# A two-layer block on one core: modulation parts ahead of the projection's first half, and two more dense steps ahead of each query chunk

## The chip, the cores and the metric

The kernel runs on one core of a Trainium2 chip. The metric is the time of one execution on the device, in microseconds. A core has TensorE (PE in the views), VectorE (DVE), ScalarE (ACT), GpSimd (POOL) and SyncE (SP), each with its own list of instructions; they wait for one another by semaphores. SP, POOL and ACT issue DMAs.

## The reference

Two transformer layers on 256 latent tokens with 256 context tokens beside them, 1024 wide, all in float32:

```python
for l in range(2):
    mx, mc = (silu(c) @ w_ada[l] + b_ada[l]), (silu(c_ctx) @ w_ada[l] + b_ada[l])   # 6 parts of 1024 each
    hx = rmsnorm(x, g0) * (1 + mx[1]) + mx[0]                                        # hc: the same with mc
    yx, yc = even_mixer(hx, hc) if l == 0 else odd_mixer(hx, hc)                     # attention, projections
    x = x + mx[2] * yx                                                               # layer 0: xc too
    h = rmsnorm(x, g1) * (1 + mx[4]) + mx[3]
    x = x + mx[5] * moe(h)                                                           # 16 experts, top 2
return rmsnorm(x, final_g)
```

Layer 0's mixer is a windowed attention (A) and a neighbourhood attention with a bias table (B), joined and multiplied by an output matrix. Layer 1's is an attention with normed and rotated queries and keys (C) and a long convolution, joined in the same way. The 6 modulation parts of a layer come from a 1024 x 6144 matrix, so they are mostly weight traffic.

## The kernel before

Each engine runs its instructions in the order in which the program writes them; nothing reorders them. The program is written as generators that are woven together: `weave(side, dense, r)` goes through an attention (`side`, two pauses per unit of 128 queries and two heads) and after each pause advances the dense work by r steps on average; `tick()` then moves on the delayed small work (`later`, and `turn_due`, which transposes a finished modulation part five ticks after its bias was added).

Weights come through `Stream W`: a list `specs` of 1 MB tiles in the order of their use, loaded by SP into a ring of 7; SP issues the next load when an older tile is used up. `order` of the list and order of the steps must agree.

The dense work beside the attentions is of three kinds. A modulation part (`g_ada`) has 4 tiles and 4 steps of 16 small matmuls; then VectorE adds the bias (`ab`, loaded by GpSimd, three buffers), GpSimd writes the row to DRAM (`mrow`) and TensorE transposes it (`adat`). An output projection (`g_out`, `op`) takes two tiles per half of its depth, 8 steps of 12 matmuls for four row tiles and two halves; each weight is split by ScalarE (high part) and VectorE (low part) and used in three products. Two weights of 512 columns fill one `pair` buffer; `Splits` keeps two ahead. The third kind are the narrow projections of layer 1's input (`qc` for the queries, `uh` for the convolution), 12 matmuls a step.

An attention unit goes: scores (`sB`, `sC`; for B also the bias table `E`), maxima and negation on VectorE (`mx`, `ng`), exponentials on ScalarE, then the scaling on VectorE, then the transposes (`tp`) of the unit before, copied out by ScalarE and VectorE (`pt`), and after the last unit of a chunk the sums (`oB`, `oC`).

In layer 0, `order_b` lists six modulation parts, (0,2), (0,4), (0,3), (0,5), (1,1), (1,0), as `ada_row(0)` to `ada_row(5)`. `fill` is the dense work beside attention B; `first` and `second` are the two halves of the projection; `ahead_first` and `ahead_out` only issue splits. After the attention follow the rest of the transposes, the shared rows of the router (`shw`), the second half of the projection, and the first expert stage (`moe`), which streams its weights.

In layer 1 each of four chunks of attention C calls `queries(c0)` first, which advances the dense work until that chunk's queries are stacked (`stackC`). Chunks 0 and 1 share one stack, and so do 2 and 3. Dense work there is: the query columns, a modulation part, the convolution's columns, `ada_row(2)`, the convolution's second half, the projection's first half, `ada_row(3)`.

Of the kernel before, what the change touches and what calls it, by code (L numbers as in the profile page):

```python
# [249 lines left out]
def tile_hybrid_flow(ctx, tc, xin, rows, adab, w_ada, w_in_e, w_out_e, sinkb, rpb, w_in_o, w_out_o, hyw,  # L250
# [50 lines left out]
    def xrow(i):  # L301

        return xt[i // 2][:, i % 2]
# [38 lines left out]
    def wtiles(ap, n, c, moe=0, kind="w"):  # L342

        return [wtile(ap, n, c, j, moe, kind) for j in range(ap.shape[1])]

    def ada_specs(l, parts, halves=(0, 1)):
        return sum([wtiles(w_ada[l], 512, 2 * q + h, kind="a") for q in parts for h in halves], [])
# [10 lines left out]
    def moe_specs(l):  # L358
        r = []
        for e in range(NE + 1):  # L360
            if e < NE:
                r += [sorted_tile(w, l, e, DE, j) for j in range(2) for w in (moe_wg, moe_wu)]
            if e:
                r += [sorted_tile(moe_wd, l, e - 1, D, j) for j in range(2)]
        return r
# [4 lines left out]
    wo = [[wtiles(w, 512, h) for h in range(2)] for w in (w_out_e, w_out_o)]  # L370
    wo = [[t[h][j] for j in range(2) for h in range(2)] for t in wo]
    specs = ada_specs(0, (1, 0), (0,)) + ada_specs(0, (1, 0), (1,))
# [1 line left out]
    specs += ada_specs(0, (2,))  # L374
    specs += ada_specs(0, (4,))
    specs += ada_specs(0, (3,))
    specs += wo[0][0:2]
    specs += ada_specs(0, (5,))
    specs += ada_specs(1, (1,))
    specs += ada_specs(1, (0,))  # L380
    specs += wo[0][2:4]
    specs += moe_specs(0)
    until_moe0 = len(specs)
    specs += cols(w_in_o, range(3)) + ada_specs(1, (2,), (0,)) + cols(w_in_o, (3,)) + ada_specs(1, (2,), (1,))
# [24 lines left out]
    def turn_due(at_once=False):  # L409

        for d in due:
            d[0] -= 1
        while due and (due[0][0] <= 0 or at_once):
            _, l, part, half, dst = due.pop(0)
            to, at = COLS[part]
            pt = tpt(f"adat{l}_{part}_{half}")
            T.transpose(pt[:, 0], dst, ident)
            V.tensor_copy(to[l][:, :, at, half * 4 : half * 4 + 4], pt[:, 0].rearrange("p (j v) -> p v j", v=32)[:, 0:2, :])
# [24 lines left out]
    def g_ada_row(order, n, pool, held):  # L443

        l, part, vs = order[n]
        for m in (n, n + 1):
            if m < len(order) and m not in held:
                if m > n:
                    turn_due(True)
                held[m] = ada_bias(*order[m][0:2], pool)  # L450
        yield from g_ada(l, part, pool, vs, bias=held.pop(n))
# [3 lines left out]
    def tick():  # L455

        for g in later[:2]:
            if next(g, later) is later:
                later.remove(g)
        turn_due()  # L460
# [9 lines left out]
    def weave(side, dense, r, whole=True):  # L470

        due = 0.0
        dense = iter(dense)
        for _ in side:
            due += r
            while due >= 1.0:
                due -= 1.0
                next(dense, None)
                tick()
        if whole:  # L480
            run(dense)

    def bcast(l, part, pool, vs, eng=G):
        t = pool.tile([P, len(vs), D], F32, name=f"bc{l}_{part}", tag=f"bc{part}")
        for a, v in enumerate(vs):
            eng.dma_start(t[:, a], mrow[l, part, v].partition_broadcast(P))
        return t
# [73 lines left out]
    class Splits:  # L561
# [25 lines left out]
        def next(self):  # L587
            self.fill()
            return self.queue.pop(0)
# [213 lines left out]
    def g_out(l, oh, ol, gate, tiles, ws, k0, lead=2):  # L803

        sp = ws if isinstance(ws, Splits) else Splits(ws, 512, lead, pool_lo=False)
        for half in range(2):
            hs = slice(half * 512, half * 512 + 512)
            grp = []
            for n, (i, ix, ig) in enumerate(tiles):
                ps = acc(f"op{l}_{half}_{k0}_{i}")  # L810
                tk = slice(i * P, i * P + P)
                for k in range(4):
                    if n == 0:
                        grp += sp.next()
                    _, hi, lo = grp[k]
                    mm3(ps, oh[k0 + k][:, tk], ol[k0 + k][:, tk], hi, lo, k == 0, k == 3)
                yield
                V.tensor_mul(ps, ps, gate(ig, half))
                V.tensor_add(xrow(ix)[:, hs], xrow(ix)[:, hs], ps)
# [798 lines left out]
    with tc.tile_pool(name="l0n", bufs=1, reuse_waits="tile") as pa:  # L1618
# [30 lines left out]
        fill = lambda n=1: [next(filters, None) for _ in range(n)]  # L1649
# [40 lines left out]
    with tc.tile_pool(name="l0q", bufs=1, reuse_waits="tile") as pq:  # L1690
# [48 lines left out]
        dense = []  # L1739
# [4 lines left out]
        dense = chain(*dense)  # L1744
# [31 lines left out]
        def chunk_b(c):  # L1776
            oh[4 + c], ol[4 + c] = htiles(pb, f"o{c}", 1, 512, f"oh{c}_") + htiles(pb, f"p{c}", 1, 512, f"ol{c}_")

            def bias(h, qt, ps):
                m0_ = 2 - 2 * (qt - 2)  # L1780
                T.matmul(ps[:, 256:512], ident, tabs[c][:, 7 * h + m0_ : 7 * h + m0_ + 4].rearrange("p m k -> p (m k)"), start=False, stop=True)

            return dict(nm=f"B{c}", q=qs[4 + c], k=ks[c], v=lambda kc, h: vB[:, kc, 128 * c + 64 * h : 128 * c + 64 * h + 64],
                        oh=oh[4 + c], ol=ol[4 + c], bias=bias, sink=None, qtiles=(0, 1, 2, 3), prep=lambda: bias_tab(c))
# [4 lines left out]
        def ada_row(n):  # L1789
            return g_ada_row(order_b, n, pe, held)  # L1790

        def reload():
            for i in range(4):
                SY.dma_start(xrow(i), xv[:, i])
            yield
# [8 lines left out]
        def ahead_first():  # L1804
            first.fill()
            yield

        def first_out():
            yield from g_out(0, oh, ol, gate0, [(i, i, i // 2) for i in range(4)], first, 0)
# [3 lines left out]
        def ahead_out():  # L1813
            second.fill()
            yield

        def gate_rows():
            gate[0] = bcast(0, 2, pb, (0, 1))
            yield

        fill = chain(ada_row(0), gate_rows(), ada_row(1), reload(), ada_row(2), ahead_first(), first_out(), ada_row(3), ada_row(4), ada_row(5), ahead_out())
        weave(g_attend(pq, [chunk_b(c) for c in range(4)]), fill, 1.26)
        turn_due(True)
    oactx.__exit__(None, None, None)
# [76 lines left out]
    with tc.tile_pool(name="l1n", bufs=1, side="right", reuse_waits="tile") as pa:  # L1901
# [27 lines left out]
        dense = chain(*[g_fm(sp, hh, hl, 256, ev_u(2 * j), f"u{j}") for j in range(4)])  # L1929
# [132 lines left out]
    def queries(c0):  # L2062

        while c0 not in stacked:
            next(dense)
            tick()

    order_c = [(1, part, (1,)) for part in (2, 4, 3, 5)]
    held = {}
# [7 lines left out]
    def fm(evac, c0, j, nm):  # L2077
        return g_fm(sp, hh, hl, 256, evac(c0 + 2 * j), f"{nm}{j}")
# [35 lines left out]
    dense = chain(g_kv(sp, hh, hl, ev_k, vt1, scr, "kvc"), fm(ev_q, 0, 0, "qc"), ada_row(1), fm(ev_q, 0, 1, "qc"), second_half())  # L2114
# [89 lines left out]
```

## Time and profile before

| | |
|---|---|
| three runs | 1147.26, 1157.21, 1153.45 us, median 1153.45 |
| the profiled execution | 1153.3 us, span 1151.4 us |
| mean granted TensorE clock | 0.944 of full speed |
| busy: PE, DVE, ACT, POOL | 1007.7, 555.5, 382.9, 146.5 us |
| moved by DMA | 328.88 MB, mean 286 GB/s |

Layer 0's attention B and what runs beside it lies at 200 to 327 us, the first expert stage from about 379; layer 1's attention C at 750 to 845, the second expert stage from about 886. In the views, idle time before an instruction stands in brackets with what ended it. A busy TensorE may still be at half its rate: the granted clock tells.

### The profile page before, as it was taken

To read this page: it belongs to the slowest core of one execution; us is meant where nothing else is said; L and a number is where in the kernel's file an instruction comes from. 1 tells how busy PE (TensorE), PEld (TensorE's weight loads), DVE (VectorE), ACT (ScalarE), POOL (GpSimd) and SP (SyncE) were. 2 spreads that over 40 slices of the span, in tenths; PEclk is the share of its full clock that TensorE was granted. 3 is DMA by queue.
4 is the path that set the end of the run, shared out by engine and by line. 5 is a ranking of instruction groups with operands and counts; after the bars stand their busy time and mean duration, and the time that the engine had idled before them with its cause. 6 is when DMAs were issued, how large, how long until landed. Compare 5 with 4: busy or idle time off the path is not lost. (4 is left out here: it accounts for less than half of the span.)

```text
span 1151.4 us, 20960 instructions
## 1 busy us (share of the span) xinstructions
PE 1007.7 (88%) x8420; PEld 555.3 (48%) x8420; DVE 555.5 (48%) x1398; ACT 382.9 (33%) x855; POOL 146.5 (13%) x176
## 2 busy tenths in 40 slices
PE   5899999889895899999997678978893999999975
PEld 2477877556573333333332376766662333333222
DVE  6565555567448543423311684467756434321114
ACT  3454454333313233333321452443342323211111
POOL 2220000210204100000001102221012100000010
PEclk9899999999996799999999889988995999999998
DMA  9932221892976899999999845345397899999993
GB/s 321 419 120 73 74 74 41 298 329 89 370 294 256 307 323 384 394 396 397 403 392 420 354 175 229 134 164 175 107 363 295 274 360 413 405 403 414 419 418 149
DMA packets 55693, 328.88 MB, mean 286 GB/s; under 512 B 8546, under 2 KB 9026, under 8 KB 21474
## 3 DMA queue, kind: packets, MB, share of 16 engines
q1 hardware_dynamic: 40179, 282.78, 62.8%
q0 software_dynamic: 10960, 32.85, 8.5%
q10 hardware_dynamic: 4448, 11.81, 2.7%
q8 instruction: 70, 1.15, 0.4%
q14 instruction: 36, 0.29, 0.1%
HBM read 315.54 MB, written 16.06 MB: 288 GB/s over the span
## 5 line engine op out<-in xcount | busy, mean ns | idle before, releaser
L1234 PE MATMUL gu<-wt,tx 128*32 128x512 f32 x2560 | 308.6, 612 | 17.4 <-DMA wt<-in_moe_wu_dram 16.1
L1234 PEld LDWEIGHTS gu<-wt,tx 128*32 128x32 f32 x2560 | 82.8, 112 | 210.1 <-issue 174.2
L1234 PE MATMUL y<-wt,hx 128*32 128x512 f32 x1280 | 147.1, 593 | 0.7 <-DMA wt<-in_moe_wd_dram 0.6
L1234 PEld LDWEIGHTS y<-wt,hx 128*32 128x32 f32 x1280 | 43.2, 110 | 96.8 <-issue 94.1
L515 DVE TENSOR_TENSOR pair<-wt,pair 128x512 fp32r<-128x512 f32 x104 | 69.0, 712 | 22.7 <-ACT pair L512 22.5
L1223 ACT ACTIVATE tx<-gp 128x192 f32<-128x192 f32 (+1 forms) x64 | 19.4, 304 | 149.2 <-PE gp L1214 120.9
L1265 DVE TENSOR_TENSOR yo<-yo,y 32x512 f32<-32x512 f32 x32 | 21.8, 683 | 90.9 <-ACT yo L1263 90.7
L512 ACT ACTIVATE pair<-wt 128x512 fp32r<-128x512 f32 x104 | 58.4, 625 | 15.6 <-DMA wt<-in_w_in_o_dram 12.3
L1275 DVE TENSOR_TENSOR he<-he,up 96x512 f32<-96x512 f32 (+1 forms) x32 | 21.9, 685 | 81.6 <-ACT up L1274 74.1
L1270 ACT ACTIVATE he<-gu 96x512 f32<-96x512 f32 (+1 forms) x32 | 19.0, 592 | 115.6 <-PE gu L1234 105.7
L1224 DVE COPY tx<-gp 128x192 f32<-128x192 f32 (+1 forms) x64 | 20.3, 323 | 74.8 <-ACT tx L1223 74.3
L429 PE MATMUL ada<-wt,siluT 128*32 128x128 f32 x1536 | 51.7, 284 | 3.6 <-ACT pt L770 2.0
L429 PEld LDWEIGHTS ada<-wt,siluT 128*32 128x32 f32 x1536 | 41.7, 113 | 16.0 <-issue 8.9
L954 POOL DMA_INDIRECT gt<-h2d,ids x16 | 15.7, 979 | 199.0 <-DVE hot L1176 92.2
L1265 DVE TENSOR_TENSOR up<-up,gu 32x512 f32<-32x512 f32 x32 | 21.9, 683 | 38.0 <-ACT up L1263 37.8
L954 POOL DMA_INDIRECT rows<-h2d,ids x16 | 15.4, 960 | 180.9 <-DVE hot L1176 104.1
L768 PE MATMUL tp<-ident,pr 128*128 128x128 f32 x256 | 33.9, 275 | 0.0
L757 DVE TENSOR_SCALAR pr<-pr,ls 128x512 f32<-128x512 f32 (+1 forms) x80 | 32.5, 457 | 1.1
L741 ACT ACTIVATE pr<-sB,ng 128x512 f32<-128x512 f32 (+1 forms) x32 | 18.2, 578 | 41.9 <-DVE ng L734 36.2
L768 PEld LDWEIGHTS tp<-ident,pr 128*128 128x128 f32 x256 | 28.7, 141 | 4.7 <-issue 2.0
L520 PE MATMUL op<-pair,oh 128*128 128x512 f32 x64 | 26.5, 414 | 3.2 <-DVE pair L515 3.1
L519 PE MATMUL op<-pair,ol 128*128 128x512 f32 x64 | 27.3, 426 | 1.7 <-ACT pair L512 1.7
(484 smaller groups left out, 1910.3 us busy)
## 6 DMA issues: line engine op xcount, KB each, us to landing
wt<-in_moe_wg_dram SPq DMA_DIRECT2D x63, 1024.0 KB
wt<-in_moe_wd_dram SPq DMA_DIRECT2D x63, 1024.0 KB
wt<-in_moe_wu_dram SPq DMA_DIRECT2D x62, 1024.0 KB
wt<-in_w_ada_dram SPq DMA_DIRECT2D x48, 1024.0 KB
wt<-in_w_in_e_dram SPq DMA_DIRECT2D x9, 1024.0 KB
wt<-in_w_in_o_dram SPq DMA_DIRECT2D x9, 1024.0 KB
ybuf<-yo ACTq DMA_DIRECT2D x16, 384.0 KB
bc<-mrow POOLq DMA_DIRECT2D x9, 512.0 KB, 10.1
```

The costliest lines, as they stand in the source:

```text
L429: T.matmul(ps[32 * j : 32 * j + 32, 0:P], siluT[:, k, :], w[:, k % 4, 128 * j : 128 * j + 128], start=(k == 0), stop=(k == KD - 1), tile_p ...
L512: newest["whi"] = S.activation(hi, w, AF.Copy).ins
L515: newest[eng] = eng.tensor_sub(lo, w, hi.bitcast(F32)).ins
L519: T.matmul(o, al, bh, start=first, stop=False)
L520: T.matmul(o, ah, bl, start=False, stop=False)
L757: V.tensor_scalar_mul(pr[:, h, at], pr[:, h, at], ls[:, h, j : j + 1])
L768: T.transpose(tp[:, kc], pr[:, h, kc * P : kc * P + P], ident)
L954: return G.indirect_dma_start(out=dst, out_offset=None, in_=h2d[l], in_offset=bass.IndirectOffsetOnAxis(ap=idx, axis=0), bounds_check=h2d[ ...
L1224: V.tensor_copy(tx[:, q * 4 + 2 : q * 4 + 4, 0:n], tp[:, 2:4, 0:n])
L1234: T.matmul(o[32 * c : 32 * c + 32], lhs, rhs, start=first, stop=last, tile_position=(0, 32 * c))
L1265: V.tensor_add(dst[q : q + 32], dst[q : q + 32], b[q : q + 32])
L1275: V.tensor_mul(he[0:n], he[0:n], up[0:n])
```

## The change

Layer 0: all six modulation parts run before the projection's first half, and the weight list follows. Layer 1: after a chunk's queries are stacked (at once, for the second chunk of a pair) two more dense steps run before its scores, eight in all.

```diff
--- before.py
+++ after.py
@@ -374,11 +374,10 @@
     specs += ada_specs(0, (2,))
     specs += ada_specs(0, (4,))
     specs += ada_specs(0, (3,))
-    specs += wo[0][0:2]
     specs += ada_specs(0, (5,))
     specs += ada_specs(1, (1,))
     specs += ada_specs(1, (0,))
-    specs += wo[0][2:4]
+    specs += wo[0]
     specs += moe_specs(0)
     until_moe0 = len(specs)
     specs += cols(w_in_o, range(3)) + ada_specs(1, (2,), (0,)) + cols(w_in_o, (3,)) + ada_specs(1, (2,), (1,))
@@ -1818,7 +1817,7 @@
             gate[0] = bcast(0, 2, pb, (0, 1))
             yield
 
-        fill = chain(ada_row(0), gate_rows(), ada_row(1), reload(), ada_row(2), ahead_first(), first_out(), ada_row(3), ada_row(4), ada_row(5), ahead_out())
+        fill = chain(ada_row(0), gate_rows(), ada_row(1), reload(), ada_row(2), ada_row(3), ada_row(4), ada_row(5), ahead_first(), first_out(), ahead_out())
         weave(g_attend(pq, [chunk_b(c) for c in range(4)]), fill, 1.26)
         turn_due(True)
     oactx.__exit__(None, None, None)
@@ -2063,6 +2062,9 @@
 
         while c0 not in stacked:
             next(dense)
+            tick()
+        for _ in range(2):
+            next(dense, None)
             tick()
 
     order_c = [(1, part, (1,)) for part in (2, 4, 3, 5)]
```

The first place is VectorE in layer 0, near the end of attention B. `ab_0_0` is the bias of the last modulation part, `pair` the low parts of the projection's weights. Before, around the last units' end:

```order
L774 COPY pt<-tp_2971 128x2x128
L774 COPY pt<-tp_2978 128x2x128
L434 TENSOR_TENSOR ab_1_0_2723<-ada_1_1_2922,ab_1_0_2723 128x128
L436 SCALAR_TENSOR_TENSOR ab_1_0_2723<-ab_1_0_2723,ab_1_1_2724 128x128
L787 TENSOR_TENSOR ol_0_1929<-oB_3006,oh_0_1928 128x256
L434 TENSOR_TENSOR ab_0_0_2862<-ada_0_0_2987,ab_0_0_2862 128x128
L418 COPY mod_100<-adat_1_0_3051 128x2x4
L434 TENSOR_TENSOR ab_0_0_2862<-ada_0_1_3032,ab_0_0_2862 128x128
L515 TENSOR_TENSOR pair<-wt,pair 128x512 x3
L418 COPY mod_100<-adat_1_1_3083 128x2x4
L418 COPY mod_100<-adat_0_0_3086 128x2x4
L418 COPY mod_100<-adat_0_1_3089 128x2x4
```

And now, around the last scores but one:

```order
L733 TENSOR_SCALAR ng<-mx 128x2
L751 RECIPROCAL ls<-ls 128x2
L756 TENSOR_SCALAR pr<-pr,ls 128x512 x2
L770 COPY pt<-tp_2845 128x2x128
L770 COPY pt<-tp_2852 128x2x128
L433 TENSOR_TENSOR ab_0_0_2580<-ada_0_1_2779,ab_0_0_2580 128x128
L514 TENSOR_TENSOR pair<-wt,pair 128x512 x3
L417 COPY mod_100<-adat_1_1_2870 128x2x4
L727 TENSOR_REDUCE mx<-sB_0_0_2873 128x2
L727 TENSOR_REDUCE mx<-sB_0_1_2874 128x2
L733 TENSOR_SCALAR ng<-mx 128x4
L514 TENSOR_TENSOR pair<-wt,pair 128x512 x3
```

The last part's bias adds and the second transposed half move ahead of the last scores' maxima (`sB_0`); the low parts of the projection's first weights stand between two softmax steps.

The second place is TensorE in layer 1, the end of attention C. Before:

```order
L782 MATMUL oC_8078<-pt,vt_6841 64x256 x8
L706 MATMUL sC_3_0_8089<-kkC,stackC 128x512
L707 MATMUL sC_3_0_8089<-klC,stackC 128x512
L706 MATMUL sC_3_1_8090<-kkC,stackC 128x512
L707 MATMUL sC_3_1_8090<-klC,stackC 128x512
L429 MATMUL ada_5_0_8106<-wt,siluT 32x128 x32
L768 MATMUL tp_8147<-ident,pr 128x128 x4
L768 MATMUL tp_8154<-ident,pr 128x128 x4
L429 MATMUL ada_5_1_8162<-wt,siluT 32x128 x32
L768 MATMUL tp_8217<-ident,pr 128x128 x4
L768 MATMUL tp_8224<-ident,pr 128x128 x4
L782 MATMUL oC_8231<-pt,vt_6841 64x256 x8
```

And now:

```order
L781 MATMUL oC_8173<-pt,vt_6841 64x256 x8
L705 MATMUL sC_3_0_8184<-kkC,stackC 128x512
L706 MATMUL sC_3_0_8184<-klC,stackC 128x512
L705 MATMUL sC_3_1_8185<-kkC,stackC 128x512
L706 MATMUL sC_3_1_8185<-klC,stackC 128x512
L767 MATMUL tp_8203<-ident,pr 128x128 x4
L767 MATMUL tp_8210<-ident,pr 128x128 x4
L767 MATMUL tp_8217<-ident,pr 128x128 x4
L767 MATMUL tp_8224<-ident,pr 128x128 x4
L781 MATMUL oC_8231<-pt,vt_6841 64x256 x8
L858 MATMUL shw_8259<-modr_102,wr_7682 16x2 x8
```

The two steps of the last modulation part (`ada_5`) stood between the last transposes (`tp`) and are gone from there; they run before the last but one scores (`sC_2_0_8141`), and nothing stands between the last scores and the sums (`oC`) but transposes.

## Rows read from the trace of the kernel before

**Rows 1.** Windows: length, busy PE, PEld, DVE, ACT, POOL; clock, DMA share, GB/s.

```profile
310.00:320.00 10.00, 4.29 (x52) 3.09 (x41) 5.01 (x17) 3.49 (x6) 4.08 (x10) 0.76 1.02 417
...
340.00:350.00 10.00, 10.00 (x54) 7.64 (x54) 4.49 (x11) 4.28 (x11) 0.00 (x0) 1.00 0.00 0
...
760.00:770.00 10.00, 7.46 (x39) 6.80 (x40) 5.96 (x14) 6.71 (x14) 0.00 (x0) 0.71 0.01 6
...
810.00:820.00 10.00, 7.17 (x35) 5.76 (x36) 7.92 (x20) 6.28 (x15) 0.00 (x0) 1.00 0.00 2
...
880.00:890.00 10.00, 3.80 (x20) 1.84 (x24) 4.60 (x21) 0.66 (x2) 2.02 (x2) 0.50 0.35 129
```

**Rows 2.** Windows, the same columns: attention of layer 0 and of layer 1.

```profile
250.00:290.00 40.00, 37.28 (x248) 26.93 (x246) 27.64 (x59) 12.72 (x35) 0.55 (x1) 1.00 0.42 132
750.00:845.00 95.00, 79.00 (x689) 63.75 (x686) 66.12 (x142) 39.01 (x90) 15.49 (x16) 0.93 0.45 159
```

**Rows 3.** Timeline of TensorE, end of layer 0's attention: start, duration, [idle before <-releaser].

```profile
314.91 0.33 PE L417 MATMUL adat<-ident,ab 128*128 128x128 f32 x1 [3.96 <-DVE mod L418]
316.99 0.47 PE L417 MATMUL adat<-ident,ab 128*128 128x128 f32 x1 [1.75 <-DVE mod L418]
...
318.50 0.63 PE L520 MATMUL op<-pair,oh 128*128 128x512 f32 x1
...
321.49 0.63 PE L521 MATMUL op<-pair,oh 128*128 128x512 f32 x1
```

**Rows 4.** Timeline of TensorE, layer 1's attention.

```profile
761.12 0.79 PE L706 MATMUL sC<-kkC,stackC 128*128 128x512 f32 x1 [4.33 <-DVE stackC L675]
...
779.02 1.77 PE L1965 MATMUL scq<-ident,wideq 128*128 128x128 f32 x8 [3.13 <-DVE pt L771]
...
798.59 1.08 PE L429 MATMUL ada<-wt,siluT 128*32 128x128 f32 x32 [2.03 <-ACT pt L770]
...
817.15 0.49 PE L519 MATMUL op<-pair,ol 128*128 128x512 f32 x1 [1.67 <-ACT pair L512]
...
835.61 1.95 PE L429 MATMUL ada<-wt,siluT 128*32 128x128 f32 x64
...
844.36 0.55 PE L859 MATMUL shw<-modr,wr 128*16 128x2 f32 x16
```

**Rows 5.** Timelines of GpSimd and VectorE, end of layer 0's attention.

```profile
306.85 0.59 POOL L404 DMA_DIRECT2D ab<-in_adab_dram  x1 [6.85 <-DMA mrow<-ab]
...
314.49 0.29 DVE L434 TENSOR_TENSOR ab<-ada,ab 128x128 f32<-128x128 f32 x1 [6.07 <-DMA ab<-in_adab_dram]
...
322.85 0.70 DVE L818 TENSOR_TENSOR op<-op,bc 128x512 f32<-128x512 f32 x1 [2.63 <-PE op L521]
```

**Rows 6.** Timeline of TensorE, layer 0's attention, second and third chunk.

```profile
231.39 1.41 PE L782 MATMUL oB<-pt,vB 128*64 128x256 f32 x8 [1.10 <-DVE pt L774]
...
243.19 2.86 PE L782 MATMUL oB<-pt,vB 128*64 128x256 f32 x16 [0.83 <-ACT pt L770]
...
248.23 1.13 PE L1781 MATMUL sB<-E,ident 128*128 128x256 f32 x4 [1.13 <-DVE E L1770]
...
252.58 0.50 PE L519 MATMUL op<-pair,o 128*128 128x512 f32 x1 [1.12 <-ACT pair L512]
```

**Rows 7.** Timelines of VectorE and ScalarE, layer 0's attention, third chunk.

```profile
248.97 1.29 DVE L728 TENSOR_REDUCE mx<-sB 128x1 f32<-128x512 f32 x2 [0.79 <-PE sB L1781]
...
252.56 1.90 DVE L515 TENSOR_TENSOR pair<-wt,pair 128x512 fp32r<-128x512 f32 x3 [2.09 <-ACT pair L512]
...
254.56 0.88 DVE L757 TENSOR_SCALAR pr<-pr,ls 128x512 f32<-128x512 f32 x2
255.36 0.75 DVE L774 COPY pt<-tp 128x256 f32<-128x256 f32 x2
...
250.56 0.69 ACT L741 ACTIVATE pr<-sB,ng 128x512 f32<-128x512 f32 x1 [4.09 <-DVE ng L734]
```

**Rows 8.** DMA issues: KB each, median us from issue to landing.

```profile
ab<-in_adab_dram POOLq DMA_DIRECT2D x16, 128.0 KB, 4.7
```

## The prediction

> **What bounds the kernel now.** I read the windows of ten microseconds first, then TensorE's timeline inside the two stretches that the change touches, then VectorE's, ScalarE's and GpSimd's timelines where TensorE stands still. The chain of waits ends in the last norm and says nothing of the middle, so it is not used.
>
> The two stretches lie each before an expert stage, and such a stage lives from its weight stream. Just before the first one starts, the DMA engines stand at 0.00 in 340 to 350, and before the second at 0.35 in 880 to 890 [rows 1]: the weight tiles have filled all the buffers there are, and the stage waits for its tokens. So a microsecond lost or won in either stretch should reach the end of the program one to one; weights that are fetched earlier win nothing, since they are already there.
>
> Inside the stretches TensorE is the engine to watch. From 250 to 290 it is idle 2.72 us of 40 [rows 2]; from 750 to 845 it is idle 16.0 us of 95 (79.00 busy) [rows 2]. The largest holes are 3.96 and 1.75 us at the end of layer 0's attention [rows 3] and 4.33 us before layer 1's first scores [rows 4]. Both have their cause in plain sight. The first: the bias of the last modulation part is asked for at 306.85 by GpSimd, which stood 6.85 us behind writes of modulation rows, and VectorE gets it at 314.49, 7.6 us after the request [rows 5]; the two transposes of that part and the second half of the projection are queued behind it. The second: the stacked queries come from a chain of small steps (square, root, scale, rotation, split) that is longer than the dense work put beside it.
>
> **The change, part by part, layer 0.** The work is the same; only its order moves. The two weight tiles of the projection's first half move behind eight tiles on SP's queue, and the modulation parts' bias loads and row writes move ahead on GpSimd's. I cost the tiles at nothing: by then the stream runs ahead of its use, and the DMA engines are busy for 0.42 of 250 to 290 [rows 2].
>
> (a) Gain at the end. The last part's steps now run in the middle of the attention, and its bias has tens of microseconds. The holes go: −3.96 −1.75 = −5.7. After them eight matmuls ran 0.43 us apart (318.50 to 321.49 are seven steps) at a granted clock of 0.76 over 310 to 320 [rows 1, 3]; at the full rate half of that goes, for nine matmuls some −1.9.
>
> (b) Small waits. Beside modulation steps (about 1 us each) TensorE waits in each chunk for the weights' transposes and for the bias table: 1.10, 0.83 and 1.13 us are such waits [rows 6]. Chunks 2 and 3 now get them too: I put 0.8 + 1.1 + 0.8 + 0.8 = 3.5. They replace 1.13 + 2.72 = 3.85 of waits beside the projection [rows 2, 6]. Net −0.35. One transpose of a part waits for VectorE to add its bias behind the softmax: +2.5 less 0.83 that is already waited there, +1.7.
>
> (c) The entry into the projection. Now it falls behind the last scores but one. Count from T, the end of these scores on TensorE. VectorE does maxima 1.29 and the negation, ScalarE two exponentials with their sums (about 1.7), VectorE the scaling 0.88, two copies 0.75, a bias add 0.28 and the low parts of three weight halves 1.9 [rows 5, 7], which with the gaps of the hand-overs is T + 6.6. Then come the next scores' maxima (T + 8) and exponentials (T + 10.1), and only behind them the low part of the fourth weight half, T + 11.4. So the first group of the projection ends near T + 12, while TensorE has about 6.2 us of work from T on: **+5.8**. A similar wait later in this half adds +1.1. At the end of the attention the second half's weights are split behind two evictions (2 × 0.70) and before the shared rows, 1.4 + 1.9 = 3.3 on VectorE [rows 5, 7], of which I let 3.0 through, since no dense work is left there.
>
> Layer 0: −5.7 − 1.9 − 0.35 + 1.7 + 5.8 + 1.1 + 3.0 = **+3.7**. The bounds of (c), the one unknown that matters: the entry before cost 1.12 us plus fractions [rows 6], with the same engines at work between two scores, so from about +1.5 to the +5.8 that I take, because the order of VectorE shows the low parts standing behind the softmax, and the row before had no second set of maxima between. Layer 0 lies between −2 and +6.
>
> **Layer 1.** Eight dense steps of 12 matmuls (1.4 us for the narrow ones) move ahead of the four query chunks' scores. Nothing is added, so what is covered early is uncovered late. Early: the four chunks now show waits of 4.33, 3.13, 2.03 and 1.67 us at or near their start [rows 4]. Two steps hide at most 2.8 of each, 2.8 + 2.8 + 2.03 + 1.67 = 9.3. But the steps themselves need split weights from the same VectorE and ScalarE that make the queries, and the rotation on GpSimd is not sped up; I take −8.1. Late: the last modulation part's two steps (1.95 us each with their neighbours [rows 4]) no longer stand between the last transposes. The last two units then run bare: maxima 1.3, negation 0.17, exponentials 1.7, reciprocal 0.16, scaling 0.88, copy 0.75, about 4.9 us a unit [rows 7], and of two units TensorE does useful work for a little: **+9.5**. Net +1.4; bounds −9.3 + 8 = −1.3, and with only the first chunk's 2.8 won, +6.7.
>
> **The clock.** TensorE's granted clock fell to 0.71 in 760 to 770, behind the 4.33 us of idling, but it stayed 1.00 in 810 to 820, with waits of 1.67 and more in it [rows 1, 4]. So the removed wait of 4.33 gives back about 2.2 us (the dense step after it ran at half its rate), the new one of 5.8 costs 1.9 as in (a), and the bare tail, with several waits of 2 to 4 us, is somewhere between nothing and the doubling of some 7 us of matmuls in it; I take +3.3. Net **+3.0**, bounds 0 and +7. The Trainium skill, "TensorE: Matmul & The Clock Gate", section "What's actually happening", says that an idle array falls to 1.2 GHz, half rate, and that activity gives 2.4 back. The 0.71 agrees; by that rule alone every new wait would be followed by slow matmuls and the bound +7 would be nearer than 3, while the 1.00 in 810 to 820 shows that a short wait need not do it.
>
> Sum: 3.7 + 1.4 + 3.0 = 8.1 us on the profiled run's 1153.3, which is also the median of the three runs (1153.45): **1161 us**.
>
> **Rivals.** *It cancels.* The entry costs 3 instead of 5.8, the tail 8 instead of 9.5, the clock nothing: 1153.3 + 8.1 − 2.8 − 1.5 − 3.0 = 1154, and 1150 to 1156 around it. For it: every term is a difference of waits that lean on each other. Chance 0.19.
>
> *Faster.* The entry costs what it cost before, about 1.5, with no later wait in this half (−5.4), the late split is hidden behind the last unit (−3.0), and the new dense steps cover the 9.3 in layer 1: 1153.3 + 8.1 − 5.4 − 3.0 − 1.2 − 3.0 (no clock loss) = 1149, and 1143 if the tail costs 4 instead of 9.5. It decides by whether the low parts get onto VectorE between two softmax steps without TensorE running dry. Against it: the order on VectorE. Chance 0.14, half of it below the 1% bound.
>
> *Clearly slower.* Every bare unit in layer 1's tail leaves TensorE at half rate, and only the first query chunk is helped: 1161 + 5.3 + 4 = 1170; 1165 to 1175. It decides at the point where the waits between the last units' transposes pass about 2 us. For it: 0.71 behind 4.33. A second way there: the bias of the last part, now due near 278. Its landing took 7.6 us with the stream at 1.02 of the DMA engines in 310 to 320, and 4.7 in the median [rows 1, 5, 8]; if the stream is as dense then, it lands as VectorE asks, or some 2 us late, and the wait stands ahead of the projection's low parts. The Trainium skill, "DMA: Bandwidth & Descriptors", section "Issuing engines are not separate DMA queues", says that transfers of all issuers share 16 engines and interleave. The 7.6 against 4.7 agrees; by it the sum would be 1163. Chance of the slower case 0.25.
>
> *The forecast* itself, 1156 to 1166, has 0.42; of it 0.07 lies above the bound.
>
> **Chances.** What three runs can tell from no change is about 1% here, 1142 to 1165. Faster: half of the faster rival, 0.07. Slower: 0.25 + 0.07 = 0.32. The same: 0.61. The range runs from 1148 (leaving out most of the faster rival) to 1172 (leaving out a part of the slower one); its ends take in layer 0's −2 and +6 and layer 1's −1.3 and +6.7.
>
> **What would show it.** In the changed profile: no wait of some 4 us on a bias at the end of layer 0's attention (a); a wait of 4 to 6 us for the low parts of a weight at the projection's first group, behind the last scores but one (c); the shared rows' product of layer 0 and the projection's second half starting 2 to 6 us later than now. In layer 1: the wait before the first scores falls from 4.33 to about 1.5; no dense matmuls after the last unit's scores, with waits of 2 to 4 us there; the shared rows' product at about layer 0's shift plus 1.4 behind 844.36 [rows 4]. The expert stages must keep their lengths, and the clock in the tail should dip below 1. Wrong would be: a first group that starts without a wait, a tail of less than 6 us of holes, or an expert stage whose length changes by more than 2 us, which would mean that the stream of weights, not the tokens, sets its start.

## The result and the profile after

The changed kernel takes 1165.69 us (median of five runs, 1161.88 to 1171.22) against 1153.45 (1147.26 to 1157.21): a ratio of 1.0115, 95% interval 1.009 to 1.0141. It is slower by 12 to 13 us. The profiled execution has a span of 1163.7 us, 12.3 more than before's, at a mean granted clock of 0.946 against 0.944.

Executions of the same program reach a given place up to some 7 us apart (the first bias table product of the attention starts between 203.61 and 210.31 in the profiles below), so I compare stretches that begin and end with the same instruction, one profile of each kernel. The first goes from that product to the shared rows' product of layer 0, the second from the wait in the query projection to the shared rows' product of layer 1. Windows of the kernel before; the columns are those of [rows 1]:

```profile
207.68:317.39 109.71, 95.76 (x1156) 66.99 (x1156) 66.78 (x165) 38.95 (x112) 18.62 (x32) 0.99 0.76 276
753.58:844.36 90.78, 75.77 (x649) 60.77 (x649) 62.46 (x136) 38.49 (x88) 12.04 (x13) 0.92 0.43 152
```

And of the kernel after:

```profile
206.90:320.99 114.09, 99.67 (x1156) 68.28 (x1156) 63.94 (x161) 35.83 (x108) 18.58 (x32) 0.97 0.80 296
758.72:858.08 99.36, 77.53 (x648) 63.29 (x649) 62.81 (x136) 38.82 (x88) 13.43 (x17) 0.90 0.54 204
```

The first stretch grew by 4.4 us, the second by 8.6. Between them and behind them nothing of that size moves: from the shared rows' product of layer 0 to the first product of the queries' norm (`scq`) in layer 1 it is 432.6 us before and 434.2 after, from the shared rows' product of layer 1 to the second expert stage's first product 41.84 and 41.16, and from there to the end 265.2 and 264.5. So the shift does pass through the expert stages.

TensorE in layer 0 after the change, the waits above one microsecond that are new, with the releaser in brackets:

```profile
243.85 0.33 PE L416 MATMUL adat<-ident,ab 128*128 128x128 f32 x1 [2.28 <-DVE pt L770]
...
286.54 0.33 PE L416 MATMUL adat<-ident,ab 128*128 128x128 f32 x1 [2.11 <-DVE pt L770]
286.80 2.08 PE L708 MATMUL sB<-k,q 64*128 64x256 f32 x8
...
293.00 0.50 PE L518 MATMUL op<-pair,o 128*128 128x512 f32 x1 [1.21 <-ACT pair L511]
...
310.01 0.50 PE L519 MATMUL op<-pair,o 128*128 128x512 f32 x1 [1.22 <-DVE pair L514]
...
323.18 0.50 PE L519 MATMUL op<-pair,oh 128*128 128x512 f32 x1 [1.21 <-DVE pair L514]
```

The bias holes of 3.96 and 1.75 [rows 3] are gone. In their place stand two waits of transposes of modulation parts (2.28 and 2.11; they come right behind an attention unit's transposes, whose two banks VectorE must first copy out), 1.21 at the entry into the projection, 1.22 and 1.21 at later weight splits, the last one behind the end of the stretch. Behind the 2.11 the scores take 2.08 us instead of the 1.13 that such products take at full rate.

TensorE in layer 1:

```profile
766.32 0.50 PE L705 MATMUL sC<-kkC,stackC 128*128 128x512 f32 x1 [1.46 <-DVE stackC L674]
...
776.52 1.16 PE L1964 MATMUL scq<-ident,wideq 128*128 128x128 f32 x8 [1.53 <-ACT wideq L1960]
...
786.02 1.08 PE L767 MATMUL tp<-ident,pr 128*128 128x128 f32 x4 [5.54 <-DVE ls L751]
...
813.37 0.50 PE L518 MATMUL op<-pair,ol 128*128 128x512 f32 x1 [2.85 <-ACT pair L511]
...
841.95 3.48 PE L781 MATMUL oC<-pt,vt 128*64 128x256 f32 x16 [3.44 <-ACT pt L769]
...
853.24 1.97 PE L767 MATMUL tp<-ident,pr 128*128 128x128 f32 x8 [5.28 <-DVE pt L770]
855.14 3.01 PE L781 MATMUL oC<-pt,vt 128*64 128x256 f32 x16
858.08 0.55 PE L858 MATMUL shw<-modr,wr 128*16 128x2 f32 x16
```

The wait before the first scores fell from 4.33 [rows 4] to 1.46 as forecast. But 5.54 us appear behind the second unit's scores, the split that cost 1.67 costs 2.85, and the tail shows 3.44 and 5.28 us with products behind them at half rate (the transposes' eight products 1.97 us, about 1.05 at full rate).

What the 5.54 hangs on, on ScalarE and VectorE:

```profile
779.78 1.28 ACT L740 ACT_TABLE_LOAD   x1 [3.31 <-DVE ng L733]
781.08 0.69 ACT L740 ACTIVATE pr<-sC,ng 128x512 f32<-128x512 f32 x1
...
782.41 0.56 ACT L1892 ACTIVATE uc<-uh,rT 128x256 f32<-128x256 f32 x1
...
783.01 0.48 DVE L1893 SCALAR_TENSOR_TENSOR uc<-uh,rT,uc 128x255 f32<-128x255 f32 x1 [3.33 <-ACT uc L1892]
...
783.93 1.28 DVE L514 TENSOR_TENSOR pair<-wt,pair 128x512 fp32r<-128x512 f32 x2
785.13 0.74 DVE L1966 SCALAR_TENSOR_TENSOR rawq<-rawq,rT,scq 128x512 f32<-128x512 f32 x1
```

ScalarE loads the table for the exponentials (1.28), does them, and only then writes the convolution's columns (`uc`, 782.41); VectorE waits 3.33 us for these, then splits a weight (783.93) and then uses the norm product `scq` (785.13 to 785.87). TensorE's transpose starts at 786.02. The reading is that `scq` held one of the two transpose banks all the while; e9 below tests it.

### The profile page after: what moved, and what is told of

Same layout as the page of the kernel before. It is cut to its first block, busy times and chain, and to the rows that moved or that the text cites. A ratio compares the mean times of both kernels' runs of the same rounds, so it can differ in the third digit from the quotient of the medians.

```text
span 1163.7 us, 20955 instructions
## 1 busy us (share of the span) xinstructions
PE 1009.6 (87%) x8420; PEld 557.3 (48%) x8420; DVE 555.9 (48%) x1398; ACT 382.1 (33%) x855; POOL 145.5 (13%) x176
## 3 DMA queue, kind: packets, MB, share of 16 engines
q8 instruction: 70, 1.15, 0.4%
## 5 line engine op out<-in xcount | busy, mean ns | idle before, releaser
L1233 PE MATMUL gu<-wt,tx 128*32 128x512 f32 x2560 | 306.7, 607 | 16.6 <-DMA wt<-in_moe_wu_dram 14.7
L1264 DVE TENSOR_TENSOR yo<-yo,y 32x512 f32<-32x512 f32 x32 | 21.8, 683 | 90.8 <-ACT yo L1262 90.6
L511 ACT ACTIVATE pair<-wt 128x512 fp32r<-128x512 f32 x104 | 58.5, 624 | 19.8 <-DMA wt<-in_w_in_o_dram 11.9
L1274 DVE TENSOR_TENSOR he<-he,up 96x512 f32<-96x512 f32 (+1 forms) x32 | 21.9, 686 | 78.9 <-ACT up L1273 78.4
L428 PEld LDWEIGHTS ada<-wt,siluT 128*32 128x32 f32 x1536 | 40.8, 111 | 13.1 <-issue 7.7
L1264 DVE TENSOR_TENSOR up<-up,gu 32x512 f32<-32x512 f32 x32 | 21.8, 683 | 37.8 <-ACT up L1262 37.6
## 6 DMA issues: line engine op xcount, KB each, us to landing
wt<-in_w_in_e_dram SPq DMA_DIRECT2D x9, 1024.0 KB, 12.8
```

The source lines that it names most:

```text
L428: T.matmul(ps[32 * j : 32 * j + 32, 0:P], siluT[:, k, :], w[:, k % 4, 128 * j : 128 * j + 128], start=(k == 0), stop=(k == KD - 1), tile_p ...
L511: newest["whi"] = S.activation(hi, w, AF.Copy).ins
L1233: T.matmul(o[32 * c : 32 * c + 32], lhs, rhs, start=first, stop=last, tile_position=(0, 32 * c))
L1264: V.tensor_add(dst[q : q + 32], dst[q : q + 32], b[q : q + 32])
L1274: V.tensor_mul(he[0:n], he[0:n], up[0:n])
```

## Experiments

Each was compared with the kernel before on its own chip. The lengths of the two stretches, from the profiles (TensorE's waits in them in parentheses; one profile of each kernel; where a stretch is the same program as before, the spread of several profiles shows what one profile can tell):

| kernel | layer 0 | layer 1 | ratio to before, 95% interval |
|---|---|---|---|
| before | 109.7 (13.5) | 90.8 (15.0) | |
| same program elsewhere | 107.4 to 109.0 | 90.5 to 92.9 | |
| after | 114.1 (14.2) | 99.4 (21.8) | 1.0115 (1.009 to 1.0141) |
| e1 layer 0 only | 112.6 (16.1) | 92.4 (15.7) | 1.0056 (1.0025 to 1.0086) |
| e2 layer 1 only | 109.0 (12.7) | 99.2 (21.9) | 1.0101 (1.0061 to 1.014) |
| e3 four bias buffers | 105.6 (9.7) | 90.5 (15.0) | 0.9967 (0.9942 to 0.9991) |
| e4 e2 at ratio 1.15 | 107.4 (11.3) | 99.1 (18.7) | 1.0063 (1.003 to 1.0096) |
| e5 first chunk only | 107.4 (11.3) | 95.5 (18.7) | 1.0034 (1.0012 to 1.0055) |
| e6 later chunks only | 107.7 (11.5) | 105.0 (23.0) | 1.0136 (1.0091 to 1.0182) |
| e7 after, early zeroing | 114.2 (14.4) | 100.3 (21.1) | 1.0162 (1.012 to 1.0205) |
| e8 e1, later transposes | 111.6 (12.8) | 92.9 (16.4) | 1.0054 (1.0034 to 1.0074) |
| e9 e5, own bank | 107.9 (11.9) | 93.6 (16.9) | 1.002 (0.9997 to 1.0043) |
| e10 e3, own bank | 105.6 (9.9) | 87.8 (13.2) | 0.9938 (0.9915 to 0.9961) |
| e11 e10, two early steps | 105.6 (9.9) | 95.3 (18.1) | 0.9999 (0.9976 to 1.0021) |
| e12 e10, one early step | 105.6 (9.9) | 94.7 (15.2) | 0.9984 (0.9956 to 1.0013) |

### The two parts apart

`e1_layer0_only` is the change without the loop in `queries`:

```diff
-        for _ in range(2):
-            next(dense, None)
-            tick()
```

> Only the layer 0 part of the change (weight list and order of the modulation parts); layer 1 as before. Theory (new waits of TensorE in layer 0 add up and pass one to one through the first expert stage): the shared rows' product of layer 0 near 321 and layer 1's attention about 5 us later than before, +5 us in all, about 1158.5. Rival (the expert stage's weight reserve takes the shift up, all 12 us come from layer 1): within 1 us of before.

Measured: +0.56%, some 6 us, by the stretch 4.4 us over the mean of the unchanged layer 0 (108.2 over six profiles). The interval (0.25 to 0.86%) leaves out the rival's 1 us: what layer 0 loses does reach the end.

`e2_layer1_only` is the kernel before with that loop.

> Only the layer 1 part (two dense steps ahead of each query chunk's scores). Theory (dense work runs out, the last two units stand bare, TensorE at half rate between them): the second shared rows' product near 853, 8.6 us after before's 844.4, and +7 us in all, about 1160.5. Rival (most of the changed kernel's loss in layer 1 is a shift from layer 0): at most +3 us.

Measured: +1.0% (7 to 16 us), and a layer 1 stretch of 99.2 against 90.5 to 92.9, 8 us more. TensorE in the stretch:

```profile
777.41 1.09 PE L768 MATMUL tp<-ident,pr 128*128 128x128 f32 x4 [5.54 <-DVE ls L752]
...
833.23 3.48 PE L782 MATMUL oC<-pt,vt 128*64 128x256 f32 x16 [3.43 <-ACT pt L770]
...
844.48 1.93 PE L768 MATMUL tp<-ident,pr 128*128 128x128 f32 x8 [5.28 <-DVE pt L771]
...
849.27 0.55 PE L859 MATMUL shw<-modr,wr 128*16 128x2 f32 x16
```

The hole behind the second unit and the two waits of the tail are those of the full change, to a tenth of a microsecond. The two parts together give 4.4 + 8 in the stretches, and 1.0056 and 1.0101 in the runs against 1.0115 for both; within their intervals that is a sum.

### Where layer 0's loss is

`e3_four_bias_buffers` keeps every engine's list and gives the bias a fourth buffer in layer 0:

```diff
-tag="ab", bufs=3
+tag="ab", bufs=4 if l == 0 or part < 2 else 3
```

> The kernel before, with a fourth buffer for the modulation parts' biases in layer 0 and nothing moved: every engine's list of instructions stays as it was, only the last bias load no longer waits for the row writes of the part (0,5). Theory (the holes of 3.96 and 1.75 us hang on that one wait): the bias lands near 306, before its use, the holes go, and with the half-rate matmuls behind them -6 to -7.5 us, about 1146.5. Rival (the landing is slow because the weight stream fills the DMA engines, or another wait is right behind): less than 2 us gained.

Measured: -0.33% (0.9942 to 0.9991). GpSimd, VectorE and TensorE at the place of [rows 3, 5]:

```profile
296.71 0.58 POOL L404 DMA_DIRECT2D ab<-in_adab_dram  x1
...
305.33 0.29 DVE L434 TENSOR_TENSOR ab<-ada,ab 128x128 f32<-128x128 f32 x1 [0.19 <-PE ada L429]
...
309.70 0.33 PE L417 MATMUL adat<-ident,ab 128*128 128x128 f32 x1 [1.92 <-DVE mod L418]
```

The load is issued at 296.71 without waiting, and VectorE's add waits no longer for a DMA. The first hole did hang on that one wait. The second did not: a transpose still waits 1.92 us, behind a weight split on VectorE. The gain is about half of what I expected, for that reason and because in all five other profiles of the same layer 0 the two holes together were shorter than in [rows 3] (from 1.76 and 1.75 to 3.27 and 1.60), so the profile I worked from had the longest. The clock of the stretch is 1.00, but so it is in three of those five (e4, e5, e9), which still have the holes: that the half-rate matmuls went by this edit isn't shown.

`e8_later_transposes` moves, in e1, the modulation parts' transposes away from the attention's:

```diff
-due.append([DELAY, l, part, half, dst])
+due.append([DELAY + (3 if l and part < 2 else -1 if l == 0 and part == 3 else 0), l, part, half, dst])
-tag="ab", bufs=3
+tag="ab", bufs=4 if (l == 0) != (part < 2) else 3
-                if m > n:
+                if m > n and n != 3:
                     turn_due(True)
```

> As e1_layer0_only, with the modulation parts' transposes moved away from places right behind an attention unit's transposes, which hold both transpose buffers (other delays for the parts (0,3), (1,1), (1,0); a fourth bias buffer in layer 0, so that the bias load of the part after needs no forced transposes). Theory (waits of 2.28 and 2.11 us of these transposes are waits for a buffer, and they are the largest loss in layer 0): both go, 3 to 4.5 us gained on e1_layer0_only, about 1154.5. Rival (they wait for VectorE, which stays as late, so the wait moves to the next instruction): no gain.

Measured: 1.0054 against e1's 1.0056, no gain that the runs can tell; the stretch is 1.0 us shorter. The waits of 2.28 and 2.11 are gone. TensorE at the entry, in e1 and then in e8:

```profile
288.61 0.33 PE L416 MATMUL adat<-ident,ab 128*128 128x128 f32 x1 [2.11 <-DVE pt L770]
...
294.96 0.50 PE L518 MATMUL op<-pair,o 128*128 128x512 f32 x1 [2.66 <-ACT pair L511]
295.68 0.50 PE L519 MATMUL op<-pair,o 128*128 128x512 f32 x1 [0.23 <-DVE pair L514]
```

```profile
281.99 0.50 PE L518 MATMUL op<-pair,o 128*128 128x512 f32 x1 [0.61 <-ACT pair L511]
...
283.50 0.50 PE L519 MATMUL op<-pair,o 128*128 128x512 f32 x1 [1.01 <-DVE pair L514]
...
288.65 0.50 PE L518 MATMUL op<-pair,o 128*128 128x512 f32 x1 [3.01 <-ACT pair L511]
```

In e1 the transpose and the splits wait 2.11 + 2.66 + 0.23 = 5.0 us; in e8 the splits alone wait 0.61 + 1.01 + 3.01 and another 0.23, 4.9 us. So at the entry the rival holds: VectorE and ScalarE are late there whatever stands first, and TensorE waits for them at one instruction or at another. The wait of 2.28 did go, and all waits of the stretch fell by 3.3 us; but its busy time rose by 2.2 (98.6 against 96.4), with a granted clock of 0.50 behind the wait of 3.01, so two thirds of that came back as half-rate products.

### Where layer 1's loss is

`e4_layer1_ratio` is e2 with fewer dense steps per pause, so that they last to the end:

```diff
-    weave(g_attend(pool, [chunk_c(c) for c in range(4)]), dense, 1.55)
+    weave(g_attend(pool, [chunk_c(c) for c in range(4)]), dense, 1.15)
```

> As e2_layer1_only, but the weave of layer 1's attention gives 1.15 dense steps per pause instead of 1.55, so the eight early steps come out of the middle and dense work lasts up to the last unit. Theory (bare tail is the loss): of the 8.7 us of waits in the tail about half goes, +2 to +4 us against before, about 1156.5. Rival (the early steps themselves cost: splits and queries stand in one another's way on VectorE and ScalarE at the start): no better than e2_layer1_only, +7.

Measured: +0.63%, some 7 us, as the rival has it; its interval overlaps e2's and reaches down to 3.5 us. The stretch is no shorter (99.1), though its waits fell from 21.9 to 18.7 us. Its window:

```profile
748.48:847.58 99.10, 80.38 (x649) 64.61 (x649) 60.41 (x136) 38.94 (x88) 12.38 (x13) 0.88 0.46 165
```

TensorE's busy time rose from 77.3 (e2) to 80.4 us for the same products, at a clock of 0.88: what the cover gave, half-rate products took back. The tail is covered (one wait of 2.16 us where e2 has 8.7), but the waits ahead of it are 16.6 us where e2 has 13.2. This run alone decides nothing.

`e5_first_chunk_only` and `e6_later_chunks_only` split the eight steps:

```diff
+        for _ in range(2 if c == 0 else 0):    # e5; in e6: range(0 if c == 0 else 2)
+            next(dense, None)
+            tick()
```

> The kernel before with two extra dense steps ahead of the first query chunk alone. Theory A (the loss in layer 1 is mostly the bare tail of 8.7 us): two steps less at the end leave most of the tail covered, layer 1's attention within 2 us of before's 91. Theory B (the loss is made at the start: the first chunk's two steps bring the second chunk's query chain between two softmax steps, the transposes' second buffer is held and a hole of 5.5 us comes behind the second unit's scores): the hole of about 5.5 us is there as in e2_layer1_only, the wait of 4.33 is 1.45, and layer 1's attention is 3 to 5 us longer than before.

> The kernel before with two extra dense steps ahead of the second, third and fourth chunk, none ahead of the first. Theory A: six of eight steps moved, the tail is nearly as bare as in e2_layer1_only (6 to 9 us of waits between the last two units), +5 to +7 us. Theory B: no 5.5 us hole, the 4.33 us wait stands as before, and the tail costs less than 4 us, +0 to +3 us.

Windows of the layer 1 stretch, e5 and then e6:

```profile
747.72:843.19 95.47, 76.71 (x648) 61.05 (x648) 60.11 (x136) 38.80 (x88) 12.08 (x13) 0.93 0.46 164
```

```profile
748.44:853.48 105.04, 82.03 (x649) 65.67 (x649) 62.75 (x136) 38.16 (x88) 13.38 (x17) 0.87 0.52 193
```

TensorE in e5, the waits at the place of the 5.54:

```profile
765.51 1.84 PE L1965 MATMUL scq<-ident,wideq 128*128 128x128 f32 x8 [3.07 <-ACT wideq L1961]
...
776.33 1.09 PE L768 MATMUL tp<-ident,pr 128*128 128x128 f32 x4 [5.29 <-DVE ls L752]
```

e5: +0.34%, stretch 4 us over the mean of the unchanged ones (91.6), with 1.46 before the first scores and 5.29 behind the second unit: theory B for the first chunk, as expected there. e6: +1.36% and a stretch of 105.0, with 2.45, 0.59 and 4.25 us of waits in the tail, and a clock of 0.87 over the whole stretch: theory A for the rest, and beyond its range. Both places lose; the six later steps lose more. Over before's stretch, e5 has 3.7 us more of waits and 0.9 us more of busy time, e6 8.0 and 6.3, and e2, with all eight steps, 6.9 and 1.5: the parts add neither in waits nor in half-rate products. Of e6's 8.0 us, 7.3 are the tail.

`e7_early_zeroing` takes the changed kernel and lets GpSimd zero the next stage's rows early:

```diff
+        rows1 = next_pools["rows1"] = m1.tile([P, 3, D], F32, name="rows1", tag="h2parts")
+        G.memset(rows1[:, 0:2], 0.0)
         yield from g_hyb(1, Ks[1])
...
-    rows1 = m1.tile([P, 3, D], F32, name="rows1", tag="h2parts")
-    G.memset(rows1[:, 0:2], 0.0)
+    rows1 = next_pools["rows1"]
```

> The changed kernel, with GpSimd's zeroing of the second expert stage's row buffer (1.8 us) issued some 40 us earlier, beside the projection's first half, so that it no longer runs while the last unit's softmax stands alone. Theory (GpSimd's zeroing stretches VectorE's negation from 0.17 to 2.25 us in the bare tail): the negation is 0.17 again, the last wait for the copies falls from 5.3 to 3.2 us, 2 us gained on the changed kernel, about 1163.5. Rival (the row of 2.25 us is a mark of something else): no change against 1165.7.

The row that called for it, GpSimd and VectorE in the changed kernel's tail:

```profile
848.29 1.82 POOL L2129 MEMSET rows<- 128x2048 f32 x1
...
847.94 2.25 DVE L733 TENSOR_SCALAR ng<-mx 128x2 f32<-128x2 f32 x1
```

And VectorE and TensorE in e7:

```profile
846.32 0.17 DVE L733 TENSOR_SCALAR ng<-mx 128x2 f32<-128x2 f32 x1
...
849.53 1.97 PE L767 MATMUL tp<-ident,pr 128*128 128x128 f32 x8 [3.21 <-DVE pt L770]
851.43 4.03 PE L781 MATMUL oC<-pt,vt 128*64 128x256 f32 x16
```

The negation is back at 0.17 us and the wait of 5.28 at 3.21, as expected; but 1167.22 us is no gain on 1165.69. The sums behind the wait took 4.03 us instead of 3.01 (half rate lasted longer), and between the projection's first split and its next wait 12.52 us passed instead of 11.13, at a clock of 0.86 instead of 1.00. The wait at `scq` was 3.08 instead of 1.53, as in e5, where the same instructions stand there, so all waits of the stretch fell by only 0.7 us while busy time rose by 1.6. The local reading was right, the time was not.

`e9_first_chunk_own_bank` is e5 with the norm product in the sums' bank:

```diff
-        sc = tpt("sc" + nm)
+        sc = ypt("sc" + nm).rearrange("p (a b) -> p a b", a=4)
```

> As e5_first_chunk_only, with the product that spreads the queries' norm (scq) in the attention's sum bank instead of one of the two transpose banks. Theory (the hole of 5.3 us behind the second unit's scores is a wait for a transpose bank, held by scq until VectorE, stuck behind the exponentials, has used it): the transposes there run on without that wait, and layer 1's attention is 2 to 5 us shorter than in e5_first_chunk_only (95.5). Rival (VectorE's order is the bound: the splits of the next dense step stand behind the same exponentials): the wait shows up at the next dense step and less than 1 us is gained.

Measured: +0.20% against e5's +0.34%, with overlapping intervals; stretch 93.6 against e5's 95.5. TensorE at the place:

```profile
770.73 1.16 PE L1965 MATMUL scq<-ident,wideq 128*128 128x128 f32 x8 [1.60 <-ACT wideq L1961]
...
774.02 1.04 PE L768 MATMUL tp<-ident,pr 128*128 128x128 f32 x8
778.86 0.39 PE L519 MATMUL uh<-hh,pair 128*128 128x256 f32 x1 [3.81 <-DVE pair L515]
```

The eight transposes run in one piece, without the 5.29 in the middle; the next dense step waits 3.81 for its split. So the bank was what the transposes waited for. That it gained 1.9 us isn't shown: e11 (below) runs the same layer 1 as e9 and has 95.3, 0.2 less than e5. There `scq` runs as in e5:

```profile
767.69 1.88 PE L1965 MATMUL scq<-ident,wideq 128*128 128x128 f32 x8 [3.08 <-ACT wideq L1961]
...
777.20 0.39 PE L519 MATMUL uh<-hh,pair 128*128 128x256 f32 x1 [3.54 <-DVE pair L515]
```

In e9 it waited half as long and ran at full rate, so the 1.9 us can be the clock's. VectorE's order is the bound, as the rival said.

### Together

`e10_bias_and_bank` is e3 with that line, no step moved; e11 and e12 add two and one early steps ahead of the first chunk.

> The kernel before with the four bias buffers of e3_four_bias_buffers and scq in the sum bank, no step moved. If banks are what scq waits for in the kernel before (3.13 us, released by a copy of transposes), it starts up to 1.9 us earlier, as soon as its input is there; -4 to -7 us against before, about 1145. If not: as e3_four_bias_buffers, -3.8 us.

> As e10_bias_and_bank, with two dense steps ahead of the first query chunk. If the early steps only lose by the bank, -4 to -7 us against before; if they lose by VectorE's and ScalarE's order, 2 to 4 us worse than e10_bias_and_bank.

> As e11_bias_bank_two with one dense step instead of two ahead of the first query chunk: half of the 4.33 us wait covered (1.4 us), and the second unit's scores one step earlier in the dense work. By the theory that the early steps lose by VectorE's order it lies between e10_bias_and_bank and e11_bias_bank_two; by the other it is the best of the three by 1 us.

e10 takes 1144.51 us against 1150.82 on its chip, 0.9938 (0.9915 to 0.9961): faster than both kernels. Its two stretches, and TensorE where [rows 4] had the wait of 3.13 us:

```profile
205.87:311.44 105.57, 95.40 (x1157) 66.87 (x1157) 66.88 (x165) 39.04 (x112) 17.75 (x31) 1.00 0.75 272
744.32:832.14 87.82, 74.60 (x649) 59.26 (x649) 62.02 (x136) 38.58 (x88) 12.02 (x13) 0.94 0.44 157
```

```profile
767.92 1.16 PE L1965 MATMUL scq<-ident,wideq 128*128 128x128 f32 x8 [1.28 <-ACT wideq L1961]
...
771.61 0.39 PE L519 MATMUL uh<-hh,pair 128*128 128x256 f32 x1 [0.19 <-DVE pair L515]
```

`scq` starts after 1.28 us, when its input is there, and the next dense step waits 0.19. Layer 0 is 2.6 us shorter than the mean of the unchanged one, layer 1 2.7 to 5.1 us. In the runs e10's interval overlaps e3's (0.9942 to 0.9991), so the bank's part of the gain rests on this one profile. With two early steps (e11) the gain is gone, with one (e12) nearly so: 95.3 and 94.7 us in layer 1 against 87.8. e11's median is 6.5 us above e10's, more than the 2 to 4 expected; e12's lies between the two, as the theory of VectorE's order has it. e11 has 5.0 us more of waits than e10 and 2.5 more of busy time. e12 divides the other way, 2.0 and 4.9:

```profile
744.37:839.09 94.72, 79.48 (x649) 64.23 (x649) 60.63 (x136) 38.46 (x88) 12.25 (x13) 0.89 0.43 154
```

Early dense steps lose here even with the bank out of the way. In e11 the larger part is waits for VectorE and ScalarE; in e12 it is half-rate products.

## Why the prediction came out as it did

The forecast was 1161 us, 8 us slower than before; measured are 12 to 13 us, at the upper edge of the forecast's own range (1156 to 1166) and at the lower one of the case "clearly slower" (1165 to 1175). It was right in sign, and the tail came as described, but the sum was a third short. With the clock's terms, layer 0 was put at 3.7 + 1.9 = 5.6 and came to 4.4; layer 1 was put at 1.4 − 2.2 + 3.3 = 2.5 and came to 8.6. So the shortfall is layer 1's, and nearly all of it is one step. By its steps:

- **Shifts pass one to one: right.** Both stretches' growth, 4.4 + 8.6 = 13.0, is found in the span (12.3).
- **(a) the holes go: right in kind, too large in size.** They went, but in other profiles of the same layer 0 they sum to between 3.5 and 4.9 us, not 5.71, and e3, where the second of them stays as 1.92 us, is 2.6 us shorter (108.2 to 105.6). The −1.9 for half-rate products behind them did not come: after the change, too, eight matmuls of the projection's second half run 0.43 us apart (from 324.55).
- **(b) the small waits: right.** 0.81, 1.10, 0.83, 0.81 where I put 0.8, 1.1, 0.8, 0.8, and 2.28 + 0.29 where I put 2.5.
- **(c) the entry: right in sum, wrong in place.** I put 5.8 on the projection's first group. There it was 1.4; 2.1 us more stand at the transpose ahead of it, and half-rate scores behind that. In e1, where these scores ran at full rate, the waits sum to 5.0, and in e8, without the transpose, to 4.9: one late VectorE, seen at two instructions. The wait of 1.1 in the middle (1.22) was right, the 3.0 at the end was 1.21 and half-rate matmuls. With (a) too large on one side and this on the other, it is partly luck that layer 0's sum is near.
- **Layer 1, late: right.** 3.44 + 5.28 = 8.7 for the 9.5 of the bare tail. But 2.1 of it is the zeroing on GpSimd, which I had not seen; 6.6 came by the mechanism that I gave.
- **Layer 1, early: the step that failed.** I took −8.1 for the waits that early steps cover. The stretch's waits outside the tail went from 15.0 to 21.8 − 8.7 = 13.1, so −1.9. The cover came: the waits that shrank or went gave 9.3 us, the first one 2.9. But the second chunk's query chain then met the second unit's exponentials, 5.54 us came back there and 1.9 at later splits. I had named what the steps ask of ScalarE and VectorE and put it at 1.2 us (9.3 − 8.1); it was 7.5. So the shared rows' product, which I put at 844.36 + 3.6 + 1.4 = 849.4 by layer 0's shift, came at 858.08. e5 shows the loss by itself: two steps ahead of the first chunk, 4 us. The rival "clearly slower" was nearer, with −2.8 of cover left, though for another reason. Its second way, a late bias of layer 0's last part, did not come: near 278 no instruction of VectorE waits for a DMA.
- **The clock: too small in sum.** I put −1.9 and +1.9 for layer 0, −2.2 and +3.3 for layer 1, +1.1 in all. The busy time of the same products rose by 3.9 us in layer 0 (99.7 against 95.8) and by 1.8 in layer 1 (77.5 against 75.8). The order of the work doesn't fix this term: e1 runs the same layer 0 at a clock of 1.00, 96.4 us busy. Nor does all of it reach the time: e1 has 1.9 us more of waits (16.1 against 14.2), 2.66 instead of 1.21 at the entry, so that 3.3 us less of busy time make a stretch only 1.5 us shorter. Half-rate products ahead of a wait shorten that wait.

Layer 1 by these terms: -1.9 + 8.7 + 1.8 = 8.6, the measured growth.

What stays open: why the six later steps lose more than all eight, of which only the terms are known, 8.0 us of waits and 6.3 of half-rate products; and what decides in one execution that the products behind a wait run at half rate.

## What to carry to other kernels

A step moved ahead of a wait covers it with the engine that waits, but it also puts its own small work on the engines that are waited for: count what the step asks of these before counting its cover. Where an engine waits at one instruction because another engine is late, moving that instruction away moves the wait (5.0 us in e1, 4.9 in e8). A buffer or bank of its own removes a wait that hangs on it alone (e3, e10) and not one behind which a late engine stands (e9, e11). Compare between two instructions that both kernels have, over several profiles: single holes changed by 2 us between executions of one program. Add up waits and busy time together, since the clock moves time from one to the other.

## What was not expected of the hardware

A negation of 128x2 elements took 2.25 us on VectorE instead of 0.17, and ended with GpSimd's zeroing beside it (848.29 + 1.82 = 850.11; 847.94 + 2.25 = 850.19); e7, where the zeroing runs elsewhere, has 0.17. e2 and e6, with the same overlap, have 2.22 and 2.15. The Trainium skill, "Advanced Engine Details and Errata", section "Mode Summary", says that VectorE's second memory port is shared with GpSimd, and that GpSimd's instructions and VectorE's two-port instructions block each other. The rows agree in that the negation lasts until the zeroing ends; no run here shows in which mode the negation ran. Not every instruction of VectorE is held up: in e7 six weight splits of 128x512 took 3.70 us from 810.33, 0.62 each, the first of them beside the same zeroing (810.30 to 812.11).

The same waits did not give the same clock. e1 and the changed kernel have the same instructions in layer 0, and up to the second transpose behind the wait of 2.28 us they also agree in time (37.57 us from the stretch's start after, 37.56 in e1). The next sums ran at half rate after, at a granted clock of 0.50, and at full rate in e1, at 1.00:

```profile
245.71 3.63 PE L781 MATMUL oB<-pt,vB 128*64 128x256 f32 x16
```

```profile
249.11 1.95 PE L781 MATMUL oB<-pt,vB 128*64 128x256 f32 x16
```
